# A third group of SwiGLU columns by seven products, with another order of the products

## The chip, the core and the metric

The kernel runs on one core of one Trainium2 chip. The metric is the device time of one execution in microseconds (us). In the profile PE is TensorE (matmuls; PEld are its weight loads), DVE is VectorE, ACT is ScalarE, POOL is GpSimd, and SP is SyncE, which here only issues DMA transfers.

## The reference

The reference is a bidirectional encoder trunk of 2 layers on one sequence of 256 tokens with 1024 channels, float32. What matters here, per layer:

```
x = x + 1/2 * SwiGLU_1(RMSNorm(x))
x = x + attention(RMSNorm(x) @ W_in) @ W_out       # two head groups, not touched here
x = x + 1/2 * SwiGLU_2(RMSNorm(x))
SwiGLU(h) = (silu(h @ w_gate) * (h @ w_up)) @ w_down   # 1024 -> 2816 -> 1024
```

So there are four SwiGLUs in an execution. Each reads some 35 MB of weights once.

## The kernel before, in words

**Precision.** A float32 product is made from three faster ones. Every operand is split in a high part, rounded to the matmul's type, and a low part, the rest. One product is high x high, low x high and high x low. For weights, ACT makes the high part (a cast) and DVE the low part (a subtraction): `emit_split`, L182. A step of 512 rows by 512 columns (1 MB) is split in two halves, so it costs two casts and two subtractions of 128 x 1024.

**Steps and look-ahead.** All weights are a list of steps (`specs`) in the order in which they are used. A step loads its megabyte into one of six raw buffers (`N_RAW`), through SP's queue. It is then split into tiles with the tag w, of which there are 14, that is seven halves with a high and a low tile each. Each call of `weights()` (L239) takes the next step, and ahead of its matmuls it issues (`ahead`, L218) the splits of what lies three steps (six halves) further on, and the loads and the preparations beyond. The instructions of the SwiGLUs keep the program's order on each engine, so a place in this text is a place in the engine's queue.

**Groups of columns.** The 2816 hidden columns are done in groups of 512 (0 to 4) and a rest of 256. A plain group uses two steps each for gate and up (upper and lower 512 rows) and does 96 matmuls of 128 x 512 for both halves of the tokens. Between them stand the transposes of the previous group's hidden tile (`turn`), and after them the down projection of that previous group: two steps of 24 matmuls, into four PSUM banks that stay in use over the whole SwiGLU. PSUM has eight banks (`bank`, L71), so four remain for all else.

**Groups by seven products.** Groups 2 and 4 (`SEVEN`, L31) use Strassen's scheme in Winograd's form (`seven`, L115, and `by_seven`, L601). The tokens' two halves and the channels' two halves make a 2 x 2 block matrix x, and the weights another: a = upper gate, d = lower gate, b = upper up, c = lower up. Seven products of 12 matmuls (`prod`) take the place of eight, so 84 matmuls of 96. The sums of x are made once per SwiGLU, during group 1 (`make_sums`). The sums of the weights are made in the raw buffers, partly by DVE (`plus`, two additions of 128 x 1024) and partly by an accumulating transfer that POOL issues (`gather`). The order of the steps is

```
a; b+c; a+b+c; down block 0; d; a+b+c+d; a+b; c; down block 1
```

Here b+c is b with c gathered onto it. For a+b+c DVE adds a, after which b is gathered into a's buffer. For a+b+c+d DVE adds a+b+c to d. The products, called P1 to P7 in this document by their names in `by_seven` (p1 to p7), use them as P1: a, P7: b+c, P6: a+b+c, P2: d, P4: a+b+c+d, P5: a+b, P3: c. They are put together by DVE in tmp tiles of 128 x 512: m1 = P1 (a copy by ACT), u2 = P6 - m1, u3 = P7 + u2, g0 = P2 + m1, and so on. silu of the two gate parts is done by ACT, and `up` (DVE) makes the two parts of the hidden tile.

Of the kernel before, what the change touches and what calls it, by code (L numbers as in the profile page):

```python
# [9 lines left out]
F32 = mybir.dt.float32  # L10
F32R = mybir.dt.float32r
AF = mybir.ActivationFunctionType
ALU = mybir.AluOpType
# [14 lines left out]
AHEAD = 10  # L28
N_RAW, N_W = 6, 14
N_S4 = 14  # L30
SEVEN = (2, 4)  # L31


@with_exitstack
def trunk(ctx: ExitStack, tc: tile.TileContext, x, n1, g1, u1, d1, nm, w_in, sink,
# [31 lines left out]
    def nm_(s):  # L67
        uid[0] += 1
        return f"{s}_{uid[0]}"

    def bank():  # L71
        return ps.tile([P, 512], F32, tag="ps", bufs=8, name=nm_("ps"))

    def halves(b):
        return b.rearrange("p (a n) -> p a n", a=2)

    def blk(dt=F32R):
        return s4.tile([P, 2, 512], dt, tag="s4", name=nm_("s4"))

    def tmp(tag="tmp", bufs=5, shape=(P, 2, 256), dt=F32):  # L80
        return tp.tile(list(shape), dt, tag=tag, bufs=bufs, name=nm_(tag))
# [24 lines left out]
    def rows(w, c0, n, k0=0, kn=None):  # L106
        kn = (w.shape[0] // P if kn is None else kn)
        return w[k0 * P:(k0 + kn) * P, c0:c0 + n].rearrange("(k p) n -> p k n", p=P)
# [6 lines left out]
    def seven(wg, wu, c0, downs):  # L115

        a, b, c, d = [object() for _ in range(4)]
        w = {a: rows(wg, c0, 512, 0, 4), b: rows(wu, c0, 512, 0, 4), c: rows(wu, c0, 512, 4, 4), d: rows(wg, c0, 512, 4, 4)}  # L120

        def load(k):
            return lambda t: [(t, w[k])]

        def gather(k, to):
            def add():
                pool.dma_start(raws[to], w[k], accum_op=ALU.add)
            return add

        def plus(x, to):  # L130
            def prep():
                for h in (0, 2):
                    x_, t_ = [raws[i][:, h:h + 2] for i in (x, to)]
                    dve.tensor_tensor(t_, t_, x_, op=ALU.add)
            return prep

        def both(*fs):
            def prep():
                for f_ in fs:
                    f_()  # L140
            return prep

        n = dict(kn=4, n=512, moves=None)
        return [Step(4, 512, load(a), key=a, free=[]),
                Step(4, 512, load(b), key=b, behind=gather(c, b), free=[]),
                Step(**n, prep=both(plus(a, b), gather(b, a)), src=b, free=[]),
                downs[0],
                Step(4, 512, load(d), key=d, free=[]),
                Step(**n, prep=plus(b, d), src=d, free=[b, d]),
                Step(**n, src=a),  # L150
                Step(4, 512, load(c), key=c),
                downs[1]]

    def emit_dma(i):
# [84 lines left out]
    def weights(less=0, held=False):  # L239

        i = at["use"]
        at["use"] += 1
        if i > 1:
            ahead(2 * i + HALVES - less)
        w = loaded[i]
        w.held = held
        return w

    for l in range(DEPTH):
        def ffn_specs(wg, wu, wd):  # L250
# [3 lines left out]
            for g in range(1, NGRP):  # L254
                downs = [down(g - 1, h) for h in range(2)]
                if g in SEVEN:
                    specs.extend(seven(wg[l], wu[l], g * 512, downs))
# [153 lines left out]
    norm = Norm(0)  # L411
# [157 lines left out]
    def ffn(norm, aside=None, before=None, final=False):  # L569
        def silu(out_, acc, t):  # L570
            act.activation(out_, acc, AF.Silu, scale=norm.r[:, t:t + 1])
            return out_

        def gate(gs):
            g = []
            for t in range(2):
                n = gs[t].shape[1]
                g.append(silu(tmp().rearrange("p a n -> p (a n)")[:, :n], gs[t], t))
            return g

        def up(h, acc, g, t):
            n = acc.shape[1]
            dve.scalar_tensor_tensor(h[:, t, :n], in0=acc, scalar=norm.hr[:, t:t + 1], in1=g, op0=ALU.mult, op1=ALU.mult)

        def hidden(g, us):
            h = blk(F32)
            for t in range(2):
                up(h, us[t], g[t], t)
            return h

        def prod(xo, w):
            acc = bank()
            for k in range(4):
                hi, lo = w.part(k)
                xh, xl = xo(k)
                pe.matmul(acc, lhsT=xh, rhs=hi, start=k == 0, stop=False)
                pe.matmul(acc, lhsT=xl, rhs=hi, start=False, stop=False)
                pe.matmul(acc, lhsT=xh, rhs=lo, start=False, stop=k == 3)
            return acc

        def by_seven(h, g):  # L601


            flat = lambda: tmp().rearrange("p a n -> p (a n)")

            def put(o, x, y, op):
                dve.tensor_tensor(o, x, y, op=op)
                return o

            p1 = prod(norm.quarter(0, 0), weights())  # L610
            m1 = flat()
            act.copy(m1, p1)
            p7 = prod(norm.summed(2), weights(2, True))
            hT = turn(h, 2)
            p6 = prod(norm.summed(1), weights())
            u2 = put(flat(), p6, m1, ALU.subtract)
            u3 = put(flat(), p7, u2, ALU.add)
            down(hT, g - 1, 0, weights())
            h = blk(F32)
            p2 = prod(norm.quarter(0, 1), weights())  # L620
            g0 = put(m1, p2, m1, ALU.add)
            w = weights()
            silu(g0, g0, 0)
            p4 = prod(norm.quarter(1, 1), w)
            g1 = put(flat(), p4, u3, ALU.subtract)
            w = weights()
            silu(g1, g1, 1)
            p5 = prod(norm.summed(0), w)
            put(u3, u3, p5, ALU.subtract)
            put(u2, u2, p5, ALU.subtract)  # L630
            w = weights()
            up(h, u3, g1, 1)
            p3 = prod(norm.summed(3), w)
            put(u2, u2, p3, ALU.add)
            w = weights()
            up(h, u2, g0, 0)
            down(hT, g - 1, 1, w)
            return h

        def turn(hs, n):  # L640
            out_ = []
            for i in range(n):
                sl = halves(bank())
                for c in range(2):
                    for t in range(2):
                        pe.transpose(sl[:, c, t * P:(t + 1) * P], hs[:, t, (2 * i + c) * P:(2 * i + c + 1) * P], ident)
                hb = blk()
                split(hb, sl)
                out_.append(hb)
            return out_  # L650

        accs = [[bank(), bank()] for _ in range(2)]

        def down(hT, g, h, w):
            tokens(accs[h], [None] * (2 * g) + hT, w, 4 * g, last=(FC - 1, G4 - 1) if final and h else FC - 1)


        gs, us = [bank(), bank()], [bank(), bank()]
        if before is None:
            before = norm.late  # L660
        before(0)
        ws = (weights(), weights(2))
        for k in (0, 2):
            if k:
                before(1)
            for sl, w in zip((gs, us), ws):
                tokens(sl, norm.xs, w, 0, (k, k + 1))
        before(2)
        tokens(gs, norm.xs, weights(), 4)
        g = gate(gs)  # L670
        tokens(us, norm.xs, weights(), 4)
        h = hidden(g, us)
        for n in range(1, NGRP):
            sums = norm.make_sums() if n + 1 == min(SEVEN, default=0) else iter(())
            if n == 3 and aside is not None:
                aside()
            if n in SEVEN:
                h = by_seven(h, n)
                continue
            gs = [bank(), bank()]  # L680
            tokens(gs, norm.xs, weights(), 0)
            hT = turn(h, 2)
            tokens(gs, norm.xs, weights(), 4)
            g = gate(gs)
            next(sums, None)
            us = [bank(), bank()]
            for k0 in (0, 4):
                tokens(us, norm.xs, weights(), k0)
                next(sums, None)
            h = hidden(g, us)  # L690
            for hh in range(2):
                down(hT, n - 1, hh, weights())
                if hh == 0:
                    next(sums, None)

        gu = [bank(), bank()]
        tokens(gu, norm.xs, weights(), 0)
        hT = turn(h, 2)
        tokens(gu, norm.xs, weights(), 4)
        h = hidden(gate([b[:, 0:256] for b in gu]), [b[:, 256:512] for b in gu])  # L700
        return accs, hT, lambda: turn(h, 1)
# [279 lines left out]
    for l in range(DEPTH):  # L981
# [7 lines left out]
        if not final:  # L989
            norm = Norm((l + 1) * 8)  # L990
# [71 lines left out]
```

## Time and profile before

| | us |
|---|---|
| three runs | 941.69, 942.12, 942.36 (median 942.12) |
| the profiled execution | 942.07 |
| its span, first to last instruction | 940.3 |
| PE busy | 929.6 (99%) |
| DVE busy | 722.2 (77%) |
| ACT busy | 539.1 (57%) |
| share of the 16 DMA engines, q1 (loads by SP) and q0 (by POOL) | 52.9% and 10.5% |

In the profile's rows of groups stand the line, the engine, the operation, what is written and read (names without buffer numbers: w is a split weight tile, raw a raw buffer, s a block of activations, q and v the sums of x, ps a PSUM bank, tmp a scratch tile), the shapes and the count, then busy time in all, the mean in ns, and the engine's idle time before them with what ended it. Nearly all instructions have line L50, the helper that records them. In the rows in order of time stand start, length, engine, instruction, how often it follows itself, and in brackets the idle time before. The end of an instruction in these rows is modelled and reaches a little into the next one, so the time between two starts says what an instruction costs in a full queue.

### The profile page before, as it was taken

The page shows a single profiled execution, that of the slowest core. Times are in us where ns is not written, and L with a number is a line of the kernel's source. Part 1 is how long each engine was busy: PE and PEld are TensorE (multiplying, and loading weights), DVE is VectorE, ACT ScalarE, POOL GpSimd, SP SyncE. Part 2 cuts the span into 40 slices and gives each one's busy share as a digit, 9 for nine tenths or more (in the row PEclk, how much of TensorE's full clock was granted, in tenths as well). Part 3 has the DMA queues.
Part 4 walks back from the last instruction along what each step waited for, and adds up shares of the span by engine and source line. Part 5 has one row for each costly group of instructions (what it writes and reads, how often), then busy time and mean ns, then how long its engine had stood idle before and what let it go on. Part 6 is the DMA issues. An engine that isn't in the chain of part 4 may idle for free.

```text
span 940.3 us, 12909 instructions
## 1 busy us (share of the span) xinstructions
PE 929.6 (99%) x4844; PEld 790.5 (84%) x4844; DVE 722.2 (77%) x1062; ACT 539.1 (57%) x829; POOL 41.3 (4%) x65
## 2 busy tenths in 40 slices
PE   8999999999999999999999999999999999999997
PEld 6888888899888888888888888888999888888886
DVE  6789869679856689769667996796796667996792
ACT  6746647467735546547464464655685464464652
POOL 0400000000000000000000000000000000000001
PEclk9999999999999999999999999999999999999999
DMA  9968948746423938948757387696642457498621
GB/s 338 347 163 283 286 117 286 239 161 167 135 77 136 277 75 283 282 124 293 238 185 224 90 300 238 167 315 184 180 140 90 135 178 225 90 321 239 171 98 45
DMA packets 106670, 186.20 MB, mean 198 GB/s; under 512 B 3438, under 2 KB 31152, under 8 KB 106608
## 3 DMA queue, kind: packets, MB, share of 16 engines
q1 hardware_dynamic: 96816, 167.27, 52.9%
q0 software_dynamic: 8704, 17.07, 10.5%
q10 hardware_dynamic: 1088, 1.05, 0.3%
q8 instruction: 38, 0.62, 0.3%
q14 instruction: 24, 0.20, 0.1%
HBM read 184.32 MB, written 1.05 MB: 197 GB/s over the span
## 4 chain that ended last, share of the span: by engine, by line
PE 96%; DVE 1%; issue 1%; ACT 1%; DMA 0%; ACTq 0%; POOLq 0%; POOL 0%; DVEq 0%
PE ps L50 96%; ACT w L50 1%; DVE w L50 0%; DMA xk<-in_x_dram 0%; DVE s L50 0%; DVE tmp L50 0%; DVE distA L50 0%; ACT tmp L50 0%; DVE distB L50 0%; DVE xk L50 0%; ACTq L50 0%; POOLq L1057 0%; POOL rf L50 0%; DVE lsum L50 0%; DVE rf L50 0%
## 5 line engine op out<-in xcount | busy, mean ns | idle before, releaser
L50 PE MATMUL ps<-w,s 128*128 128x512 f32 (+1 forms) x2994 | 691.0, 390 | 0.1
L50 PEld LDWEIGHTS ps<-w,s 128*128 128x128 f32 x2994 | 557.7, 188 | 114.5 <-DVE s L50 0.7
L50 DVE TENSOR_TENSOR w<-raw,w 128x1024 fp32r<-128x1024 f32 (+1 forms) x416 | 440.8, 1089 | 113.8 <-ACT w L50 110.4
L50 ACT CAST w<-raw 128x1024 fp32r<-128x1024 f32 (+1 forms) x416 | 373.3, 941 | 173.1 <-PE ps L50 126.0
L50 PE MATMUL ps<-s,w 128*128 128x256 f32 x672 | 84.0, 285 | 0.0
L50 PEld LDWEIGHTS ps<-s,w 128*128 128x128 f32 x672 | 81.7, 191 | 1.1
L50 PE MATMUL ps<-w,q 128*128 128x512 f32 x288 | 70.1, 392 | 0.0
L50 PEld LDWEIGHTS ps<-w,q 128*128 128x128 f32 x288 | 53.5, 188 | 10.7
L50 ACT CAST s<-ps 128x512 fp32r<-128x512 f32 x48 | 26.0, 589 | 47.3 <-PE ps L50 47.3
L50 DVE TENSOR_TENSOR s<-ps,s 128x512 fp32r<-128x512 f32 x48 | 31.1, 687 | 26.9 <-ACT s L50 26.9
L50 PE MATMUL ps<-ident,s 128*128 128x128 f32 x304 | 39.6, 273 | 0.0
L50 PEld LDWEIGHTS ps<-ident,s 128*128 128x128 f32 x304 | 35.1, 141 | 4.7
L50 DVE TENSOR_TENSOR raw<-raw,raw 128x1024 f32<-128x1024 f32 x32 | 37.7, 1221 | 0.0
L50 POOL DMA_DIRECT2D raw<-in_ffn_w_up_dram x16 | 20.8, 1298 | 380.1 <-DVE tmp L50 118.5
L50 ACT ACTIVATE s<-s,negm 128x256 f32<-128x256 f32 x64 | 31.9, 500 | 6.6 <-DVE negm L50 6.6
L50 ACT CAST q<-tmp 128x512 fp32r<-128x512 f32 x20 | 12.4, 619 | 35.0 <-DVE tmp L50 35.0
L50 DVE SCALAR_TENSOR_TENSOR s<-ps,gcol,s 128x256 fp32r<-128x256 f32 x48 | 20.3, 479 | 15.0 <-ACT s L50 14.9
L50 ACT ACTIVATE s<-ps,gcol 128x256 fp32r<-128x256 f32 x48 | 19.2, 473 | 21.2 <-PE ps L50 21.2
L50 ACT ACTIVATE tmp<-tmp,r 128x512 f32<-128x512 f32 x16 | 11.6, 726 | 31.7 <-DVE tmp L50 31.7
L50 ACT ACTIVATE tmp<-ps,r 128x512 f32<-128x512 f32 (+1 forms) x32 | 19.8, 635 | 15.5 <-PE ps L50 15.4
L50 DVE TENSOR_TENSOR tmp<-tmp,s 128x256 f32<-128x256 f32 x56 | 23.4, 425 | 1.6
L50 PE MATMUL ps<-w,v 128*128 128x512 f32 x96 | 23.1, 389 | 0.0
(106 smaller groups left out, 416.5 us busy)
## 6 DMA issues: line engine op xcount, KB each, us to landing
raw<-in_ffn_w_down_dram SPq DMA_DIRECT2D x44, 1024.0 KB, 5.2
raw<-in_ffn_w_gate_dram SPq DMA_DIRECT2D x39, 1024.0 KB, 5.3
raw<-in_ffn_w_up_dram SPq DMA_DIRECT2D x39, 1024.0 KB, 5.3
raw<-in_ffn_w_up_dram POOLq DMA_DIRECT2D x16, 1024.0 KB, 9.1
raw<-in_w_in_dram SPq DMA_DIRECT2D x14, 1024.0 KB, 5.2
raw<-in_ffn_w_gate_dram SPq DMA_DIRECT2D x8, 512.0 KB, 3.7
raw<-in_ffn_w_up_dram SPq DMA_DIRECT2D x8, 512.0 KB, 4.8
raw<-in_w_in_dram SPq DMA_DIRECT2D x8, 512.0 KB, 5.0
```

The source lines that it names most:

```text
L50: ins = issue(*a, **k)
```

## The change

Groups 2, 3 and 4 go by seven products, not only 2 and 4. In all of them the order of the steps becomes

```
a; b+c; d; down block 0; a+b; a+b+c; c; a+b+c+d; down block 1
```

The sums grow in a's buffer: b is gathered into it by a transfer once a is split, DVE then adds c, and later d. The products come in the order P1, P7, P2, P5, P6, P3, P4, with the transposes of the previous hidden tile after P7, as before.

```diff
-SEVEN = (2, 4)
+SEVEN = (2, 3, 4)
...
-                Step(4, 512, load(b), key=b, behind=gather(c, b), free=[]),
-                Step(**n, prep=both(plus(a, b), gather(b, a)), src=b, free=[]),
+                Step(4, 512, load(b), key=b, behind=gather(c, b), prep=gather(b, a)),
+                Step(4, 512, load(d), key=d, free=[]),
                 downs[0],
-                Step(4, 512, load(d), key=d, free=[]),
-                Step(**n, prep=plus(b, d), src=d, free=[b, d]),
-                Step(**n, src=a),
-                Step(4, 512, load(c), key=c),
+                Step(4, 512, load(c), key=c, src=a, free=[]),
+                Step(4, 512, None, prep=plus(c, a), src=a, free=[]),
+                Step(4, 512, None, src=c),
+                Step(4, 512, None, prep=plus(d, a), src=a, free=[a, d]),
                 downs[1]]
...
             p7 = prod(norm.summed(2), weights(2, True))
             hT = turn(h, 2)
+            p2 = prod(norm.quarter(0, 1), weights())
+            g0 = put(flat(), p2, m1, ALU.add)
+            w = weights()
+            silu(g0, g0, 0)
+            down(hT, g - 1, 0, w)
+            h = blk(F32)
+            p5 = prod(norm.summed(0), weights())
             p6 = prod(norm.summed(1), weights())
             u2 = put(flat(), p6, m1, ALU.subtract)
             u3 = put(flat(), p7, u2, ALU.add)
-            down(hT, g - 1, 0, weights())
-            h = blk(F32)
-            p2 = prod(norm.quarter(0, 1), weights())
-            g0 = put(m1, p2, m1, ALU.add)
-            w = weights()
-            silu(g0, g0, 0)
-            p4 = prod(norm.quarter(1, 1), w)
-            g1 = put(flat(), p4, u3, ALU.subtract)
+            v3 = put(m1, u3, p5, ALU.subtract)
+            put(u2, u2, p5, ALU.subtract)
+            p3 = prod(norm.summed(3), weights())
+            put(u2, u2, p3, ALU.add)
+            up(h, u2, g0, 0)
+            p4 = prod(norm.quarter(1, 1), weights())
+            g1 = put(u3, p4, u3, ALU.subtract)
             w = weights()
             silu(g1, g1, 1)
-            p5 = prod(norm.summed(0), w)
-            put(u3, u3, p5, ALU.subtract)
-            put(u2, u2, p5, ALU.subtract)
-            w = weights()
-            up(h, u3, g1, 1)
-            p3 = prod(norm.summed(3), w)
-            put(u2, u2, p3, ALU.add)
-            w = weights()
-            up(h, u2, g0, 0)
+            up(h, v3, g1, 1)
             down(hT, g - 1, 1, w)
             return h
```

More of the change, by code (lines that the diff above doesn't have):

```diff
@@ L135, in plus @@
             return prep
[L137 to L143, printed above, removed]
         return [Step(4, 512, load(a), key=a, free=[]),
-                Step(4, 512, load(b), key=b, behind=gather(c, b), free=[]),
-                Step(**n, prep=both(plus(a, b), gather(b, a)), src=b, free=[]),
+                Step(4, 512, load(b), key=b, behind=gather(c, b), prep=gather(b, a)),
+                Step(4, 512, load(d), key=d, free=[]),
                 downs[0],
-                Step(4, 512, load(d), key=d, free=[]),
-                Step(**n, prep=plus(b, d), src=d, free=[b, d]),
-                Step(**n, src=a),
-                Step(4, 512, load(c), key=c),
+                Step(4, 512, load(c), key=c, src=a, free=[]),
+                Step(4, 512, None, prep=plus(c, a), src=a, free=[]),
+                Step(4, 512, None, src=c),
+                Step(4, 512, None, prep=plus(d, a), src=a, free=[a, d]),
                 downs[1]]
```

## The prediction

> **What bounds the kernel now.** I read the page's busy times first, then its groups, then the stretches of the three groups of columns, then the order of time on TensorE (PE) and VectorE (DVE) through one group.
>
> ```profile
> PE 929.6 (99%) x4844; PEld 790.5 (84%) x4844; DVE 722.2 (77%) x1062; ACT 539.1 (57%) x829; POOL 41.3 (4%) x65
> L50 DVE TENSOR_TENSOR w<-raw,w 128x1024 fp32r<-128x1024 f32 (+1 forms) x416 | 440.8, 1089 | 113.8 <-ACT w L50 110.4
> L50 DVE TENSOR_TENSOR raw<-raw,raw 128x1024 f32<-128x1024 f32 x32 | 37.7, 1221 | 0.0
> ```
> ```profile
> 352.35:383.18 30.83, 30.83 (x142) 25.62 (x141) 29.55 (x32) 20.54 (x24) 0.00 (x0) 1.00 0.85 279
> 383.18:416.72 33.54, 33.54 (x153) 27.86 (x152) 21.79 (x21) 15.47 (x17) 2.57 (x2) 1.00 0.76 200
> 416.72:447.54 30.82, 30.82 (x142) 25.61 (x141) 28.14 (x30) 20.00 (x22) 0.00 (x0) 1.00 0.78 266
> ```
>
> PE is busy for 99% of the span, so time goes only where matmuls go, or where PE begins to wait. The second fence holds the stretches of the second SwiGLU from the transposes of one group to those of the next (length; then PE, weight loads, DVE, ACT, POOL; clock; DMA share). The first covers most of group 2, the second most of plain group 3, the third most of group 4. PE is dense in each, but DVE is busy for 29.55 of 30.83 us around group 2 and 28.14 of 30.82 around group 4; in the plain stretch it has 12 us to spare. Before, a plain group always follows a seven-product group. After, three follow each other.
>
> **What the change removes.** Group 3's 96 gate and up matmuls become 84, in four SwiGLUs: 48 fewer.
>
> ```profile
> 416.72 1.03 PE L50 MATMUL ps<-ident,s 128*128 128x128 f32 x8
> 417.51 2.98 PE L50 MATMUL ps<-w,q 128*128 128x512 f32 x12
> 420.33 11.04 PE L50 MATMUL ps<-w,s 128*128 128x512 f32 x48
> 431.21 2.88 PE L50 MATMUL ps<-w,q 128*128 128x512 f32 x12
> 433.93 2.88 PE L50 MATMUL ps<-w,v 128*128 128x512 f32 x12
> 436.65 11.05 PE L50 MATMUL ps<-w,s 128*128 128x512 f32 x48
> 447.54 1.04 PE L50 MATMUL ps<-ident,s 128*128 128x128 f32 x8
> ```
>
> From 420.33 to 431.21 PE does 48 matmuls in 10.88 us, 0.2267 us each; one product (12) is 2.72 us (431.21 to 433.93). The 48 that go are worth **-10.88 us**, all on the path.
>
> **What it adds to DVE.** By the built program's lists, DVE gets 68 more instructions: per new seven-product group 6 splits of weights, 4 additions in raw buffers and 7 operations on products. ACT gets 28 (24 casts, 4 copies of P1), POOL eight accumulating transfers; SP's 186 stay 186. Here is how long DVE takes from one start to the next:
>
> ```profile
> 417.98 1.29 DVE L50 TENSOR_TENSOR s<-ps,s 128x512 fp32r<-128x512 f32 x2 [3.00 <-ACT s L50]
> 419.41 2.36 DVE L50 TENSOR_TENSOR w<-raw,w 128x1024 fp32r<-128x1024 f32 x2
> 421.69 2.36 DVE L50 TENSOR_TENSOR raw<-raw,raw 128x1024 f32<-128x1024 f32 x2
> 424.08 2.38 DVE L50 TENSOR_TENSOR w<-raw,w 128x1024 fp32r<-128x1024 f32 x2
> 426.38 1.41 DVE L50 TENSOR_TENSOR tmp<-ps,tmp 128x512 f32<-128x512 f32 x2
> 427.71 4.62 DVE L50 TENSOR_TENSOR w<-raw,w 128x1024 fp32r<-128x1024 f32 x4
> 432.25 0.69 DVE L50 TENSOR_TENSOR tmp<-ps,tmp 128x512 f32<-128x512 f32 x1
> 432.85 1.22 DVE L50 TENSOR_TENSOR w<-raw,w 128x1024 fp32r<-128x1024 f32 x1
> 434.67 1.22 DVE L50 TENSOR_TENSOR w<-raw,w 128x1024 fp32r<-128x1024 f32 x1 [0.60 <-ACT w L50]
> 435.81 0.68 DVE L50 TENSOR_TENSOR tmp<-ps,tmp 128x512 f32<-128x512 f32 x1
> 441.69 0.75 DVE L50 SCALAR_TENSOR_TENSOR s<-tmp,hr,tmp 128x512 f32<-128x512 f32 x1
> 442.36 1.22 DVE L50 TENSOR_TENSOR w<-raw,w 128x1024 fp32r<-128x1024 f32 x1
> ```
>
> A seven-product group needs: 18 splits at 1.14 us (20.5), 4 additions at 1.17 (4.7), the eviction of the transposes 1.43 (417.98 to 419.41), 7 product operations at 0.60 to 0.66 (4.4), two hidden tiles at 0.67 (1.3): 32.3 us, and 33.5 with the two gaps of 0.60 behind ACT's silu. PE's period for one is 30.82. Before, the plain neighbour absorbs this; in a run of three it cannot.
>
> **What the other order of the products does.** This decides. PSUM has eight banks; four hold the sums of the down projection, four remain. In the old order P6 follows the transposes, and P7 and P6 are read soon after. In the new one P7 lies in its bank until u3 = P7 + u2, u2 = P6 - m1 waits for P6, and P5 waits for both. When PE comes to P4, the four banks hold P7, P5, P6 and P3; the built program has P4's first matmul wait for u2, which frees P6's bank. u2 stands in DVE's queue, by program order, behind the eviction of the transposes, then the splits of a+b (2), the additions of c (2), the splits of a+b+c (2), g0, the splits of c (2), the additions of d (2), the splits of a+b+c+d (2) and of the second down block (2), because each call for weights issues what lies three steps ahead. DVE counted from the transposes' start, T = 416.72:
>
> eviction begins and ends 417.98 to 419.41, so the a+b splits start at T + 2.69; 2.28 (419.41 to 421.69); 2.39 for two additions (421.69 to 424.08); 2.30 (424.08 to 426.38); g0 0.60 (432.25 to 432.85); c's splits with ACT's gap 2.96 (432.85 to 435.81); 2.39; four splits 4.54 (427.71 to 432.25); u2 0.69. The sum is 18.15, so u2 ends at **T + 20.84**.
>
> PE counted from T: transposes 0.79, P2 2.82 (417.51 to 420.33), then 60 matmuls (down block, P5, P6, P3) at 0.2267, 13.60: P4 could start at **T + 17.21**. PE waits **3.63 us**, in every seven-product group, the eight old ones too: 12 x 3.63 = +43.6. The splits that PE needs meanwhile come earlier (those of c end at T + 13.2 and P3 starts at T + 14.5; those of a+b+c+d end 2.97 us before u2, at T + 17.9), so this wait ends last. It doesn't grow from group to group: the period becomes 34.45, DVE's need is 33.5, and DVE has again 0.95 us of idle time before the next transposes. Group 2 begins alike, since the old addition of a ahead of its transposes is gone.
>
> **Steps with no or little cost.** The transfer b into a no longer waits behind an addition and starts once a is split; some 11.4 us later (product operations 1.3, hidden tiles 1.3, six splits 6.8, gap 0.6, idle 0.95, eviction 1.43, less a cast of 0.98) ACT wants a+b:
>
> ```profile
> raw<-in_ffn_w_up_dram POOLq DMA_DIRECT2D x16, 1024.0 KB, 9.1
> DMA to landing us min/median/max: 8.1/9.1/15.1
> raw<-in_ffn_w_gate_dram SPq DMA_DIRECT2D x39, 1024.0 KB, 5.3
> 437.16 4.83 ACT L50 CAST w<-raw 128x1024 fp32r<-128x1024 f32 x5
> ```
>
> The median 9.1 is covered; 15.1 is not (a rival, below). On POOL's queue this transfer stands ahead of the next group's c into b, as before. The five casts give 0.97 each. The loads on SP wait in its queue for raw buffers in another order (the next a takes b's buffer, the next c that of a), but each has most of a group for a landing of 5.3 us: nothing. ACT's 28 more instructions fill idle time. In the first SwiGLU the attention constants, which group 3 covered, now fall into a full DVE queue:
>
> ```profile
> 100.66 0.19 DVE L50 COPY gcol<-ps 128x34 f32<-128x34 f32 x1
> 104.08 0.14 DVE L50 TENSOR_SCALAR gsub<-gcol 128x1 f32<-128x1 f32 x1
> 108.43 1.28 ACT L50 ACT_TABLE_LOAD   x1
> ```
>
> They take DVE from 100.66 to 104.22, 3.56 us, less 0.95 idle: 2.6; the table load of 1.28 delays a silu, between 0 and 1.28, taken as 0.9 because c's cast runs beside it. **+3.5**.
>
> **Sum.** 940.3 - 10.88 + 43.6 + 3.5 = 976.5 of span; the profiled execution took 942.07, 1.77 beside its span, so **978.3 us** (its time stands 0.05 under the median of the runs, 942.12).
>
> **Rivals.**
> - *The wait is hidden, only the matmuls count.* 942.07 - 10.88 = **931.2**, faster. It needs a wait under 10.88 / 12 = 0.91 us, that is DVE 2.7 us sooner at u2, more than two splits of weights. For it: PE never waits in the old seven-product groups. Against: the order of DVE's queue is fixed and each length is a row. 0.06.
> - *The bank is no limit, DVE's throughput is.* Then PE loses 32.3 - 30.8 = 1.5 us per group, or 2.7 with the gaps: 931.2 + 18 to 931.2 + 32, about **949 to 963**. For it: the splits run ahead of PE by some microseconds. 0.13.
> - *Late transfers as well.* In groups 3 and 4 DMA has little idle time (0.85 of it busy above); a landing of 13.5 instead of 11.4 would add 2.1 us to eight groups, **995**. 0.11.
> - *A cold PE after each wait.* The trace shows it once, at the start:
>
> ```profile
> 3.38 0.26 PE L50 MATMUL ps<-ident,grow 16*128 16x16 f32 x1 [3.38 <-DMA grow<-in_ffn_norm_dram]
> 6.16 7.66 PE L50 MATMUL ps<-w,s 128*128 128x512 f32 x24
> 13.66 1.04 PE L50 MATMUL ps<-ident,xk 128*128 128x128 f32 x8
> 0.00:6.00 6.00, 1.98 (x8) 1.50 (x9) 0.82 (x2) 2.58 (x4) 0.90 (x8) 1.00 0.64 198
> ```
>
> After the idle first microseconds 24 matmuls took 7.50 us (6.16 to 13.66) and not 24 x 0.2267 = 5.44, though the granted clock reads 1.00: 2.06 us lost. If each of the twelve waits did this, 978.3 + 24.7 = **1003**. The waits are about as long as PE's idle at the start (3.38 before its first instruction), hence 0.10 and not more. [...]
>
> **Chances and range.** Forecast 0.60 (its own range 966 to 990: the wait 2.7 to 4.6 us, if gaps, idle time or transfers are off by a microsecond), hidden 0.06, throughput 0.13, late 0.11, cold 0.10. The range 960 to 1004 takes in the forecast, both dearer rivals and the dear end of the throughput case, and leaves out under 0.2. A change under 0.2% can't be told from none here: slower 0.93, same 0.01, faster 0.06.
>
> **What would show it.** On PE a gap of 3 to 4 us before P4 in each of twelve groups (weight load or matmul of the products from the s tiles, released by DVE tmp), period near 34.4 from transposes to transposes; no gap elsewhere; DVE without idle time from the eviction of the transposes to u2; 12 matmuls after the gap at 2.72 us (cold: above). Wrong would be: gaps in front of P5 (late transfers) or spread over splits (throughput), or none.

## The result, and the profile after

The changed kernel takes **1001.33 us** (median of four runs, 1000.04 to 1003.58), the kernel before 941.98 on the same chip. The ratio is 1.063, with a 95% interval of 1.061 to 1.065: slower by 59 us. The profiled execution took 1000.95 with a span of 999.2, so the trace has 58.9 us more than that of before (940.3).

The page's busy times and two of its groups, and the waits of PE (what is waited for, total us, how often, the longest), and the span with the mean granted clock:

```profile
PE 944.1 (94%) x4796; PEld 796.0 (80%) x4796; DVE 787.3 (79%) x1130; ACT 566.7 (57%) x857; POOL 51.1 (5%) x73
L50 PE MATMUL ps<-w,s 128*128 128x512 f32 (+1 forms) x2754 | 661.3, 400 | 44.5 <-DVE tmp L50 44.4
raw<-in_ffn_w_up_dram POOLq DMA_DIRECT2D x24, 1024.0 KB, 8.7
```
```profile
PE ps L50 <- DVE tmp L50: 44.4, 12, 4.1
```
```profile
core 0: 999.2 us, clock 0.973
```

PE has its 48 matmuls fewer (4796, not 4844), but is busy for 14.5 us more. It waits twelve times for a tmp tile of DVE, 44.4 us in all; the others that the view lists, 4.0 us, are at the kernel's start. And the granted clock is 0.973 on the mean, where full speed would be 1. One group of the second SwiGLU on PE, in order of time, from its transposes at 366.84 to those of the next at 403.18, and on to the next wait:

```profile
366.84 1.03 PE L50 MATMUL ps<-ident,s 128*128 128x128 f32 x8
...
381.32 2.88 PE L50 MATMUL ps<-w,v 128*128 128x512 f32 x12
387.85 12.76 PE L50 MATMUL ps<-w,s 128*128 128x512 f32 x48 [3.65 <-DVE tmp L50]
400.45 2.89 PE L50 MATMUL ps<-w,q 128*128 128x512 f32 x12
403.18 1.03 PE L50 MATMUL ps<-ident,s 128*128 128x128 f32 x8
...
424.19 2.13 PE L50 MATMUL ps<-w,s 128*128 128x512 f32 x7 [3.63 <-DVE tmp L50]
```

The row at 387.85 begins with P4, and the wait in its brackets is the one in front of P4. The same row hides the second loss: from 387.85 to 400.45 PE needs 12.60 us for 48 matmuls, which took 10.88 in the kernel before. DVE in the group that begins at 403.18:

```profile
404.43 1.29 DVE L50 TENSOR_TENSOR s<-ps,s 128x512 fp32r<-128x512 f32 x2 [2.92 <-ACT s L50]
...
418.81 4.64 DVE L50 TENSOR_TENSOR w<-raw,w 128x1024 fp32r<-128x1024 f32 x4
423.36 1.41 DVE L50 TENSOR_TENSOR tmp<-ps,tmp 128x512 f32<-128x512 f32 x2
```

The last row begins with u2, at 423.36, behind four splits of weights. PE starts P4 at 424.19, one operation of DVE later. From the transposes' eviction (404.43) to there is DVE's queue as the prediction counted it.

The clock, by stretches (from:to, length, then busy us of PE, PEld, DVE, ACT and POOL, the granted clock, the DMA share and GB/s): the wait of group 2, three stretches behind it, and then the surroundings of two other waits, in group 4 of the second SwiGLU and in group 3 of the last:

```profile
384.10:387.85 3.75, 0.10 (x1) 0.03 (x1) 3.71 (x5) 3.75 (x5) 0.00 (x0) 1.00 1.05 397
387.85:389.50 1.65, 1.65 (x4) 1.27 (x5) 1.62 (x3) 0.45 (x1) 0.00 (x0) 0.56 1.04 382
389.50:391.00 1.50, 1.50 (x5) 1.20 (x4) 1.50 (x3) 0.83 (x1) 0.00 (x0) 0.50 1.07 393
391.00:393.00 2.00, 2.00 (x9) 1.60 (x9) 1.96 (x3) 0.98 (x2) 0.68 (x1) 0.88 0.78 287
457.00:469.00 12.00, 8.44 (x25) 6.78 (x26) 11.90 (x15) 6.10 (x7) 0.00 (x0) 0.72 0.97 353
916.00:928.00 12.00, 8.99 (x40) 7.48 (x41) 11.90 (x14) 6.11 (x7) 1.28 (x1) 1.00 0.90 284
```

Soon after PE resumes, the clock is at half: 0.56, 0.50, then 0.88 as it comes back. In the trace's own records of the clock this drop lasts 3.41 us. Behind the wait of the next row (457 to 469) the mean of 0.72 over 12 us stands for a half clock of 6.7 us (0.28 x 12 / 0.5; 6.83 in the records). Eleven of the twelve waits end in such a drop, seven of 3.41 us and four of 6.83; only the wait that ends at 919.01 (last row) has none.

So the 58.9 us are: 48 matmuls fewer, -10.9; twelve waits, +44.4; eleven stretches at half clock, +23.6 (seven of 3.41, in which PE is busy throughout, lose half of it, 11.9 together; four of 6.83, in which PE is still idle at first, lose 2.8 to 3.0 each, 11.7 together); and a rest of 1.8 that no run explains.

### The profile page after: what moved, and what is told of

It is laid out like the page before. It is cut to its first block, busy times and chain, and to the rows that moved or that the text cites. A ratio compares the mean times of both kernels' runs of the same rounds, so it can differ in the third digit from the quotient of the medians.

```text
span 999.2 us, 12985 instructions
## 1 busy us (share of the span) xinstructions
PE 944.1 (94%) x4796; PEld 796.0 (80%) x4796; DVE 787.3 (79%) x1130; ACT 566.7 (57%) x857; POOL 51.1 (5%) x73
## 4 chain that ended last, share of the span: by engine, by line
PE 77%; DVE 11%; ACT 7%; issue 5%; DMA 0%; ACTq 0%; POOLq 0%; POOL 0%; DVEq 0%
PE ps L50 77%; DVE w L50 6%; ACT w L50 6%; DVE raw L50 3%; DVE tmp L50 1%; ACT s L50 1%; DMA xk<-in_x_dram 0%; DVE s L50 0%; ACTq L50 0%; ACT tmp L50 0%; DVE distA L50 0%; ACT L50 0%; DVE xk L50 0%; DVE distB L50 0%; POOLq L1048 0%
## 5 line engine op out<-in xcount | busy, mean ns | idle before, releaser
L50 PE MATMUL ps<-w,s 128*128 128x512 f32 (+1 forms) x2754 | 661.3, 400 | 44.5 <-DVE tmp L50 44.4
L50 PEld LDWEIGHTS ps<-w,s 128*128 128x128 f32 x2754 | 526.6, 194 | 159.9 <-ACT w L50 49.9
L50 DVE TENSOR_TENSOR w<-raw,w 128x1024 fp32r<-128x1024 f32 (+1 forms) x440 | 466.7, 1095 | 88.2 <-ACT w L50 85.1
L50 ACT CAST w<-raw 128x1024 fp32r<-128x1024 f32 (+1 forms) x440 | 398.1, 946 | 198.4 <-PE ps L50 127.1
L50 PE MATMUL ps<-w,q 128*128 128x512 f32 x432 | 101.9, 389 | 0.0
L50 PEld LDWEIGHTS ps<-w,q 128*128 128x128 f32 x432 | 81.1, 188 | 16.8
L50 DVE TENSOR_TENSOR raw<-raw,raw 128x1024 f32<-128x1024 f32 x48 | 56.5, 1219 | 0.0
L50 PE MATMUL ps<-w,v 128*128 128x512 f32 x144 | 34.6, 389 | 0.0
L50 DVE TENSOR_TENSOR tmp<-ps,tmp 128x512 f32<-128x512 f32 x48 | 32.9, 686 | 0.4
L50 DVE SCALAR_TENSOR_TENSOR s<-ps,gcol,s 128x256 fp32r<-128x256 f32 x48 | 20.3, 478 | 14.6 <-ACT s L50 14.5
L50 PEld LDWEIGHTS ps<-w,v 128*128 128x128 f32 x144 | 27.0, 188 | 5.6
```

Of the source, the lines that this page charges most:

```text
L50: ins = issue(*a, **k)
```

## Experiments

**The order alone.** The changed kernel, but only groups 2 and 4 by seven products:

```diff
-SEVEN = (2, 3, 4)
+SEVEN = (2, 4)
```

> The changed kernel with groups 2 and 4 only, so the new order alone. If the wait for the bank ahead of P4 comes from the order (my theory), it is there in all 8 groups, 3.6 us each and about 2 us of half clock behind it: 942 + 8 x 5.6 = 987. If three groups in a row make it, because DVE's work overflows (rival), plain group 3 absorbs it and the time is about 942.

Measured: 989.2 us (one run). PE's row of P4 in group 2 of the second SwiGLU, and its waits:

```profile
385.10 15.50 PE L50 MATMUL ps<-w,s 128*128 128x512 f32 x60 [3.64 <-DVE tmp L50]
```
```profile
PE ps L50 <- DVE tmp L50: 29.2, 8, 3.7
```

The wait is there in full although the neighbour of each such group is plain. So it is the order of the products that makes it, not the third group. The kernel gains nothing of the 48 matmuls and loses 47 us.

**The third group alone.** The kernel before with its old order, but with three groups:

```diff
-SEVEN = (2, 4)
+SEVEN = (2, 3, 4)
```

> The kernel before with groups 2, 3 and 4, so the number of groups alone. Theory (order): no wait for a bank ahead of a product; the 48 matmuls are gained, less what DVE's 33.5 us per 30.8 us cost in groups 3 and 4, up to 3 us per SwiGLU: 931 to 945. Rival (three in a row): waits in all four SwiGLUs as in the changed kernel, 970 or more.

Measured: 991.82 us (988.46 to 993.75), ratio 1.052 (1.050 to 1.054). This missed by 50 us: the old order cannot do groups in a row either, for another reason. Rows of one group, from SP's load of b to the transposes; each row names its engine:

```profile
374.15 0.37 SPq L159 DMA_DIRECT2D raw<-in_ffn_w_up_dram  x1
```
```profile
379.74 1.28 POOL L50 DMA_DIRECT2D raw<-in_ffn_w_up_dram  x1 [17.40 <-DMA raw<-in_ffn_w_up_dram]
```
```profile
393.09 2.00 ACT L50 CAST w<-raw 128x1024 fp32r<-128x1024 f32 x2 [4.83 <-PE ps L50]
```
```profile
394.17 1.23 DVE L50 TENSOR_TENSOR w<-raw,w 128x1024 fp32r<-128x1024 f32 x1 [3.45 <-ACT w L50]
...
401.12 0.75 DVE L50 SCALAR_TENSOR_TENSOR s<-tmp,hr,tmp 128x512 f32<-128x512 f32 x1
```
```profile
401.92 1.09 PE L50 MATMUL ps<-ident,s 128*128 128x128 f32 x8 [3.48 <-DVE s L50]
```

In the old order b's buffer holds b, b+c and a+b+c in turn and comes free only with a+b+c+d, so the next group's b is loaded late, and the accumulating transfer that needs it (POOL, 379.74) lands only some 13 us later. ACT's cast at 393.09 waits for it; the row names PE as what released it, but PE's part was long done. DVE stands 3.45 us behind that cast, with the hidden tile's last operation (401.12) in its queue, and the transposes wait for the hidden tile. Eight such waits (27.1 us) and again a lower clock (0.977 on the mean of a span of 986.7 us, so some 22.7 us of it are missing) make most of the loss. In the changed kernel, where the sums grow in a's buffer, the view names no transfer for any wait of PE but those at the start.

**A seventh raw buffer for the old order.** To settle that cause: the same kernel, one raw buffer more (and two tiles of the tag s fewer, for room).

```diff
-N_RAW, N_W = 6, 14
-N_S4 = 14
+N_RAW, N_W = 7, 14
+N_S4 = 12
```

> The old order with three groups, with seven raw buffers in place of six (and 12 activation blocks in place of 14, to make room). In the run with six, the next group's b was loaded only when b's buffer was free after a+b+c+d, and c gathered onto it landed 13 us later, past its need. With seven buffers b's load starts some 8 us sooner. If that is the cause of the 3.5 us waits at the transposes, they go: 945 to 970. If DVE's full queue is the cause, they stay: 985 or more.

Measured: 954.86 us (one run).

```profile
PE ps L50 <- DVE s L50: 9.7, 7, 1.9
```

The waits fall from 27.1 us (8 of them) to 9.7 (7), and the time by 37 us. The late load was the cause of most of it; what sets the 9.7 us that are left was not tried.

**P7 off its bank.** The changed kernel, but ACT copies P7 to a tmp tile at once, so that its bank does not wait for u2.

```diff
             p7 = prod(norm.summed(2), weights(2, True))
+            u3 = flat()
+            act.copy(u3, p7)
...
-            u3 = put(flat(), p7, u2, ALU.add)
+            put(u3, u3, u2, ALU.add)
```

> The changed kernel, but ACT copies P7 to a scratch tile right after it, so its bank is free long before P4. Theory (bank): the twelve waits released by u2 go, and with them the half clock; what stays is DVE's throughput, 0 to 3 us per group in groups 3 and 4: 935 to 955. Rival (the splits themselves are late): waits of the same length stay, now ended by the splits, about 1000.

Measured: 959.34 us (958.89 to 959.70), ratio 1.018 (1.016 to 1.020), some 4 us outside what was expected.

```profile
392.51 8.50 PE L50 MATMUL ps<-w,s 128*128 128x512 f32 x36 [1.28 <-ACT tmp L50]
...
424.48 0.98 PE L50 MATMUL ps<-ident,s 128*128 128x128 f32 x7 [0.76 <-DVE s L50]
```
```profile
PE ps L50 <- ACT tmp L50: 12.5, 8, 4.5
PE ps L50 <- DVE s L50: 4.1, 8, 0.8
```

All twelve waits for u2 are gone, and the granted clock is 0.992 on the mean in place of 0.973; the time falls by 42 us. A bank that is held for a late sum was what PE waited for. In their place stand short waits. ACT copies P1 and P7 only behind silu and its casts, so P2 waits 1.28 us for a bank, and the hidden tile comes late for the transposes.

**The half clock.** In the changed kernel the product P3, which runs ahead of the wait, is done twice into the same bank: 144 matmuls more in all, so that PE arrives later at the same wait. The second run of the twelve restarts the sum in the bank, so the output is the same.

```diff
-        def prod(xo, w):
+        def prod(xo, w, times=1):
...
-            for k in range(4):
+            for k in list(range(4)) * times:
...
-            p3 = prod(norm.summed(3), weights())
+            p3 = prod(norm.summed(3), weights(), 2)
```

> The changed kernel with the 12 matmuls of P3 done twice into the same bank (the second run restarts the sum, so the output is the same): 144 matmuls more, 2.72 us of work per group, put where PE waits. If the slow matmuls behind the wait are the clock falling after an idle stretch (theory), the wait shrinks to 0.9 us, the clock stays at 1.00 and the time falls by some 23 us to about 977. If they are slow for another cause (the banks or the weights' memory), the time stays near 1001; if P4 waits for something other than DVE's u2, it grows by up to 33 us.

Measured: 980.17 us (one run).

```profile
419.17 11.14 PE L50 MATMUL ps<-w,s 128*128 128x512 f32 x48 [0.92 <-DVE tmp L50]
```
```profile
core 0: 978.4 us, clock 0.999
```
```profile
PE ps L50 <- DVE tmp L50: 11.8, 12, 1.4
```

144 matmuls more, and 21 us less. The wait shrinks by what the twelve matmuls take, which by itself gains nothing. What is gained is the clock: 0.999 on the mean in place of 0.973, and the 48 matmuls from 419.17 on have the old pace (11.14 in their row, 11.04 in a row of the kernel before). So the half clock costs the changed kernel some 21 us, against 23.6 by the count above.

**u2 sooner in DVE's queue.** P6's call for weights looks one half less ahead, and no more splits are issued until P3's call. So the two splits of the second down block come behind u2, not ahead of it.

```diff
-            p6 = prod(norm.summed(1), weights())
+            p6 = prod(norm.summed(1), weights(1, True))
```

> The changed kernel, but the call for P6's weights looks one half less ahead and holds that until P3, so the splits of the second down block come behind u2 in DVE's queue. Theory: u2 comes two splits (2.28 us) sooner, P4 waits 1.35 us instead of 3.63 in all twelve groups, and a wait that short leaves the clock at 1.00: 942 - 10.9 + 12 x 1.35 + some 3 = 950. If the clock falls after any wait (rival), 20 us more, 970; if P4 waits for something else, about 1000 as before.

Measured: 966.96 us (965.47 to 970.85), ratio 1.027 (1.024 to 1.029), 17 us more than expected.

```profile
381.03 11.20 PE L50 MATMUL ps<-w,s 128*128 128x512 f32 x48 [1.37 <-ACT w L50]
...
414.81 12.57 PE L50 MATMUL ps<-w,s 128*128 128x512 f32 x48 [2.34 <-ACT w L50]
```

```profile
380.20 1.41 DVE L50 TENSOR_TENSOR tmp<-ps,tmp 128x512 f32<-128x512 f32 x2
...
398.76 2.36 DVE L50 TENSOR_TENSOR w<-raw,w 128x1024 fp32r<-128x1024 f32 x2 [0.61 <-ACT w L50]
...
413.98 1.41 DVE L50 TENSOR_TENSOR tmp<-ps,tmp 128x512 f32<-128x512 f32 x2
```

In group 2 the wait falls by 2.28 us, two splits (3.65 to 1.37), so the place in the queue sets it. PE's rows name ACT's cast of P4's weights as the releaser, but u2 ends last in both groups: it begins at 380.20 and 413.98, and P4 starts 0.83 us after that, as in the changed kernel (423.36 and 424.19). In group 3 u2 ends later after its transposes, at T + 19.87 (T = 394.80) and not T + 18.60 (T = 362.29): DVE comes to their eviction 0.8 us later, out of a full queue, and then stands 0.61 us for the cast of a+b. That is why the wait is 2.34 us there. Behind it the 48 matmuls take 12.40 (414.81 to 427.21), behind the wait of 1.37 they take 11.04 (381.03 to 392.07). The granted clock of this run is 0.990 on the mean of a span of 963.7 us, so some 9.6 us of it are missing in all, where 1.00 was expected.

**silu behind the down block.** With P7 copied, ACT's silu moves, so that ACT is sooner at its copies.

```diff
-            w = weights()
-            silu(g0, g0, 0)
-            down(hT, g - 1, 0, w)
+            down(hT, g - 1, 0, weights())
+            silu(g0, g0, 0)
```

> P7 copied, and silu of the first gate part stands behind the casts of the first down block on ACT, so that the 0.60 us gap in DVE's queue between c's two splits goes. If DVE's throughput sets the period of groups in a row, each of the 12 groups gains up to 0.6 us: 959 to 952 to 956. If the rest is set elsewhere (ACT's copies ahead of P2, transfers): 958 to 960, no change.

Measured: 950.91 us (948.94 to 953.48), ratio 1.010 (1.008 to 1.012), 8.4 us less than with P7 copied alone and 1 us below what the theory gave. The waits for ACT's copies fall only from 12.5 to 11.6 us in all, but those for the hidden tile from 4.1 to 0.8:

```profile
PE ps L50 <- DVE s L50: 0.8, 1, 0.8
```

In the profiled executions the clock makes up most of the rest: 0.996 on the mean of 947.2 us in place of 0.992 of 957.1, so some 3.9 us less of it are missing.

**The copies ahead too.** On top of that, P1's call takes its look-ahead later (as P7's does), and the attention constants move from group 3 to ahead of the last 256 columns.

```diff
-            p1 = prod(norm.quarter(0, 0), weights())
+            p1 = prod(norm.quarter(0, 0), weights(1, True))
...
-            if n == 3 and aside is not None:
-                aside()
...
+        if aside is not None:
+            aside()
         gu = [bank(), bank()]
```

> The run with P7 copied and silu later, and two more moves: P1's call for weights leaves the casts of the next down block until after ACT's copy of P1, so that P2 finds its bank free; and the attention constants of the first SwiGLU stand ahead of the last 256 columns instead of group 3. Of that run's 12.9 us of waits, those on ACT's copies (11.6 with the 4.5 in the first SwiGLU) should go: 951 - 12 = 939, and 937 without the half clock behind the longest, faster than the kernel before by about 0.4%. If DVE's queue is what sets these waits (it is full in groups in a row), they only move, to the splits or to the transposes: 945 to 951.

Measured: 954.50 us (953.71 to 955.01), ratio 1.013 (1.011 to 1.014). The rival was right in that the waits only move, but the run takes 3.5 us more than its 945 to 951.

```profile
PE ps L50 <- DVE s L50: 8.8, 13, 0.8
PE ps L50 <- DVE w L50: 4.2, 8, 0.5
```
```profile
387.83:421.23 33.40, 31.72 (x140) 25.40 (x140) 32.44 (x34) 20.98 (x25) 2.57 (x2) 1.00 0.89 252
```

The waits for ACT's copies are gone, and the same time stands before the transposes and at P4's weights. From transposes to transposes DVE is busy for 32.44 us of 33.40.

**DVE's work.** If DVE's total is the limit there, taking work from it must help. Three runs did so. In the first, GpSimd made the low parts of the second down block (with P7 copied):

```diff
-            dve.tensor_tensor(l_, r_, f(h_), op=ALU.subtract)
+            (s.low or dve).tensor_tensor(l_, r_, f(h_), op=ALU.subtract)
...
+        downs[1].low = pool
```

> The kernel with P7 copied by ACT, and POOL instead of DVE makes the two low parts of the second down block in each seven-product group (two operations of 128 x 1024 less on DVE per group, 2.28 us, so its need falls from 33.5 to 31.2 against PE's 30.8). If DVE's throughput is what is left between the run with P7 copied (959) and the matmuls alone (931): 932 to 942, faster than the kernel before. If POOL is too slow (some 2.6 us each by its 1.28 us for half the size) or slows DVE at the same memory: 950 or more, the waits then standing in front of the second down block.

Measured: 960.17 us (958.45 to 961.33), ratio 1.019 (1.017 to 1.020): no gain. DVE has 24 operations fewer, but was busy as long as without the edit (785.6 us, and 784.5 with P7 copied alone). The waits stay at ACT's copies (13.1 us); those for GpSimd's tiles are 1.9. GpSimd's row and two of DVE's beside it:

```profile
411.79 5.32 POOL L50 TENSOR_TENSOR w<-raw,w 128x1024 fp32r<-128x1024 f32 x2 [10.03 <-ACT w L50]
```
```profile
412.65 2.18 DVE L50 TENSOR_TENSOR tmp<-tmp,tmp 128x512 f32<-128x512 f32 x1
414.86 1.28 DVE L50 TENSOR_TENSOR tmp<-tmp,ps 128x512 f32<-128x512 f32 x2
416.07 3.25 DVE L50 TENSOR_TENSOR w<-raw,w 128x1024 fp32r<-128x1024 f32 x2
```

While GpSimd's subtractions run (411.79 to 417.1), DVE's operations with two inputs from SBUF stretch: 2.18 us for one that takes 0.69 with silu behind the down block (its 376.39), 3.25 for two that take 2.36 elsewhere in this run. Those with an input from PSUM keep their time (1.28 for two, as with u2 sooner).

In the second, ACT copies the raw weights as the low part of that block in place of DVE's subtraction. This leaves a right low part out of the block; the instructions keep their number and sizes.

```diff
-            dve.tensor_tensor(l_, r_, f(h_), op=ALU.subtract)
+            if s.low:
+                act.copy(l_, r_)
+            else:
+                dve.tensor_tensor(l_, r_, f(h_), op=ALU.subtract)
...
+        downs[1].low = True
```

> P7 copied, and the low parts of the second down block of each seven-product group are made by ACT as a plain copy of the raw weights, where DVE makes a subtraction (a wrong value: the low part is the whole weight there). DVE is relieved by 2.28 us per group without POOL at its side. If DVE's throughput is what costs 959 against 931: 932 to 945. If the same waits stay in front of P2, because ACT or the transfers set them: 952 to 960.

Measured: 948.73 us (one run), 10.6 us less than with P7 copied alone, between the two theories. The waits for ACT's copies stay for the most part (8.5 us of 12.5). The third is the same edit on the kernel that had those waits removed:

> The kernel with both copies, silu later, P1's step moved and the attention constants moved (954.50 us), and in it ACT copies the raw weights as the low part of the second down block in place of DVE's subtraction. This leaves out a right low part in that block; the number of instructions stays, 24 operations of 1.14 us go from DVE to ACT. If DVE's throughput sets the period of three seven-product groups in a row (33.4 us, of which DVE is busy 32.4), DVE's need falls by 2.3 us per group to about 31.1, near PE's 30.8 without waits: about 8 groups give back some 1.5 to 2.3 us each, 937 to 943 us, at or below the kernel before (942). If the waits before the transposes come from the order of the queues and not from DVE's total work, they stay: 950 to 955.

Measured: 948.21 us (946.83 to 949.18), ratio 1.006 (1.004 to 1.008), again between the two.

```profile
384.62 1.03 PE L50 MATMUL ps<-ident,s 128*128 128x128 f32 x8
...
402.78 0.73 PE L50 MATMUL ps<-w,s 128*128 128x512 f32 x2 [0.78 <-ACT w L50]
...
417.36 1.03 PE L50 MATMUL ps<-ident,s 128*128 128x128 f32 x8
```
```profile
PE ps L50 <- ACT w L50: 6.4, 9, 1.1
PE ps L50 <- DVE s L50: 0.4, 1, 0.4
```

The waits before the transposes are gone (8.8 to 0.4 us), so they came from DVE's work. This does not part its total from its order, since two splits fewer also bring all that stands behind them sooner. The period falls from 33.40 to 32.74 us (384.62 to 417.36), not to 30.8. What is left lies in front of P4's first weights, the splits of a+b+c+d. These end a chain in one raw buffer (a split, b gathered, c added and split, d added and split), and in this run ACT's casts wait for the gather, 1.45 us at 389.42 and 1.61 at 422.40. That this chain is the next limit is argued from the place of the waits; it was not tried apart. No version beats the kernel before.

## Why the prediction was right, and where not

The time lies in the range of 960 to 1004, at its dear end, and outside the likeliest case's own range of 966 to 990. The direction and the wait came out as reasoned. That the range holds the time is owed to its having taken in a rival that was given a chance of 0.10; the forecast of 978.3 was 23 us short. The steps one by one:

- **-10.88 us for 48 matmuls.** 4796 are there, and where the clock is full they keep their pace: 12 from 400.45 to 403.18.
- **The wait of 3.63 us at P4.** Right in place, releaser, number and length: 3.65 and 3.63 in the rows above, twelve of them. u2 was to end at T + 20.84; it begins at 423.36, with T = 403.18, and one such operation of 0.69 later it is T + 20.87. Three runs show the mechanism: the order alone makes it, P7 off its bank removes it, and two splits fewer ahead of u2 shorten it by two splits in group 2.
- **Attention constants, +3.5.** Oversized for this kernel. In the first SwiGLU the waits of groups 3 and 4 are 4.07 and 3.91 in place of 3.65, together about 0.7:

```profile
128.34 12.77 PE L50 MATMUL ps<-w,s 128*128 128x512 f32 x48 [4.07 <-DVE tmp L50]
164.97 15.49 PE L50 MATMUL ps<-w,s 128*128 128x512 f32 x60 [3.91 <-DVE tmp L50]
```

With the wait at u2 gone they cost more: with P7 copied, ACT stands 2.67 us for their first sums with its copies behind it, and P2 waits 4.5 us (the longest in that run's view).

- **The transfers, 0.** Right for this kernel: they land 8.7 us after their issue (median; the latest 13.5), mostly inside the 11.4 that were worked out, and no wait on PE is put down to them.
- **PE at full speed after the wait.** This is the step that failed: the sum has nothing for it. It was the rival "a cold PE after each wait", 1003 us with a chance of 0.10, and the time is 1001. Its price was near (2.06 each, 24.7 for twelve; measured 23.6 for eleven), its chance was not. The chance was the author's estimate, and the kernel before could not show how often such a wait is followed by slow matmuls: its PE waits only in the first 6 us (3.4 us, and 0.6 in two more waits). In the changed kernel half clock came with eleven of twelve waits of 3.63 to 4.07 us. The period came out at 36.34 us (366.84 to 403.18), not 34.45.

  The prediction also read the start of the kernel before wrongly when it set a granted clock of 1.00 beside the slow matmuls there. That trace's records of the clock begin only at 10.22 us, so the 1.00 for 0 to 6 us stands for no record. From 7.23 to 10.22 the matmuls start 0.427 us apart, the pace of the half clock behind the waits, and from there on 0.23.
- **DVE's throughput, 949 to 963.** As a rival for this change it lost, since the wait at u2 ends later. Once that wait is taken away it is a part of what remains (959 with P7 copied, 951 to 955 with the copies sooner), since less work on DVE makes it less; ACT's copies and the half clock are other parts.
- **Hidden, 931.** Not seen in any run; without the wait at u2 and with less work on DVE the best still takes 948: the short waits at P2, at the transposes and at P4 take more than the 10.9 us.

## What to carry to other kernels

When products are reordered, write down for each PSUM bank which operation frees it, and count that operation's place in its engine's queue: here the wait could be told to 0.02 us from rows of the old kernel. In the changed kernel eleven of the twelve waits of 3.63 to 4.07 us on TensorE cost another 1.7 to 3.0 us each in half clock, so a wait is not to be charged with its length alone; 144 matmuls put into these waits made the run 21 us shorter. A scheme that trades matmuls for vector work is to be judged by the vector engine's need per group, not by its mean share: here 32.4 us per group against TensorE's 30.8, at a mean share of 82%.

## What the runs showed of the hardware beyond that

**Where the half clock began and ended in the changed kernel.** In the clock records of its trace the eleven drops begin and end on one grid of 3.413 us, whatever the waits do: 388.06 to 391.48, the next from 425.61, and ten steps of 3.413 lie between 391.48 and 425.61. In the step of the grid in front of each drop PE was idle for between 2.0 us (58% of it; the wait that ends at 424.19) and 3.22 us (the wait that ends at 90.91), in none for the whole of it. The one wait without a drop, from 915.38 to 919.01, was cut by the grid at 917.13 into 1.75 and 1.88 us (55% at most). The beginnings of these waits are modelled ends of matmuls, good by an estimate to some 0.15 us (the row of 48 matmuls at 420.33 of before has 11.04 us, and the next begins after 10.88). The drop lasted 3.41 us in the seven cases in which the wait had ended before it began, and 6.83 in the four in which the wait reached 0.82 to 1.20 us into it. Of the experiments' figures: with u2 sooner, 48 matmuls took 11.04 us behind a wait of 1.37 and 12.40 behind one of 2.34; with P3 twice the longest of the twelve waits for a tmp tile was 1.4 us, and the clock was 0.999 on the mean.

**While GpSimd subtracted, DVE's operations with two SBUF inputs took longer.** Beside two subtractions of 2.67 us each (the mean of 24) one took 1.5 us more and two took 0.9 more in the rows above, and moving work there gave nothing: 960.17 us, where P7 copied alone has 959.34.

**The releaser that a row names can be the wrong one of two.** The cast at 393.09 in the old order is put down to PE, and it started 13.35 us after the issue of the accumulating transfer that it needs (379.74). P4 at 381.03, with u2 sooner, is put down to a cast of ACT, and it started 0.83 us after the beginning of u2, as it does where the row names u2.
